# A two-layer decoder trunk: both feed-forward blocks in one matmul form, the residual's chunks turned a step ahead, two attention heads paired

## The chip, the cores and the metric

The kernel runs on one core of a Trainium2 chip. The metric is the device time of one execution in microseconds; the kernel before takes 2439.62 us, the median of three runs (2439.14 to 2440.86). Engines are named as the profile names them: PE is TensorE's matmuls and PEld its weight loads, DVE is VectorE, ACT is ScalarE, POOL is GpSimd, SP is SyncE, which issues the DMAs of the weights.

## What is computed

Two layers on a residual stream h of 256 positions by 2048 columns, each with three sub-layers in sandwich norms (cut from the reference):

```python
for l in range(DEPTH):                                   # DEPTH = 2
    xn = rms_norm(h, mix_pre_g[l])
    proj = jnp.einsum('bsd,dc->bsc', xn, w_in[l])
    qa, ka, va, cq, ckv, kidx, widx, cu, cv = jnp.split(proj, split_at, axis=-1)
    oa = diff_attention(...)                             # 6 heads of 128
    ob = dsa_attention(...)                              # 6 heads of 128
    oc = chunk_spatial_gating(gelu(cu), gelu(cv), ...)   # 512 columns: u * (W_s v + b)
    mix = concatenate([oa, ob, oc])
    h = h + rms_norm(jnp.einsum('bsc,cd->bsd', mix, w_out[l]), mix_post_g[l])
    xa = memory_attention(rms_norm(h, x_pre_g[l]), rms_norm(mem, mem_g[l]), ...)
    h = h + rms_norm(xa, x_post_g[l])
    ff = swiglu(rms_norm(h, f_pre_g[l]), f_w_gu[l], f_w_down[l])   # 2048 -> 2 x 5632 -> 2048
    h = h + rms_norm(ff, f_post_g[l])
```

## The kernel before

Everything stays in SBUF but the weights, which are streamed once. A matrix is used in f32 accuracy as a pair of rounded parts: hi is the value rounded to the matmul's type, lo what is left; a product is hi times hi, hi times lo and lo times hi, three matmuls. Chunks are 128 columns of h; KD is 16 of them.

The stream. plan() (from L263) lists the weights in the order of their use; loaded() lets SP load them in pieces of 1 MB, tile raw with three buffers; splits() cuts a piece into batches of 1024 elements a row, ACT copying hi (L206) and DVE subtracting for lo (L207). weights() hands batches to the matmuls. After each batch it splits ahead up to three batches (prefetch) and lets every waiting side job take one step (pump): side jobs are Python generators, appended with start(), and their steps fall where the matmuls of that batch stand in the program. Behind that, the Tile framework's scheduler fixes the order on each engine, with its own estimate of times, except where a stretch is put under manual_schedule: begin() does that for DVE and ACT from one of the residual's steps until the first weights after it are used up, and in that stretch weights() pumps first and splits ahead afterwards.

Forms of a matmul. mm_n gives rows: h's chunk is the stationary side, 512 weight columns move. mm_t gives the transposed output: a 128 by 128 block of weights is stationary and 256 positions move; a chunk and block takes lo with x's hi, hi with x's hi, and hi with x's lo, three matmuls of 256 columns with three weight loads, and four blocks (512 weight columns: two of the gate g, two of u) make a group. mm_w puts x's hi and lo side by side, so that a block's hi serves both in one matmul of 512 columns, with one of 256 for lo; the two halves of the result are added afterwards by add_up (ACT L425, DVE L427).

The feed-forward block (from L1237) takes its 5632 hidden columns in two halves of 11 groups, each group 256 hidden columns. Layer 1 and the first two groups of layer 0 go through mm_t; the other 20 groups of layer 0 through mm_w, two calls for a group, with side job act_w; its u is multiplied by the norm on POOL (L1279). g times u is POOL's (L1254).

The residual (L609) adds a normed sub-layer output og to H and turns H for the next sub-layer, two chunks at a time: turn_x (L588) transposes two chunks on PE (L593; tile xtp, one of two PSUM tiles each) and splits them (ACT L212, DVE L213, tile x). add is DVE's (L622), add_beside scales on ACT (L628) and adds on POOL (L629). Its argument bare tells that no other matmuls stand beside it: cross to FFN in both layers, FFN to the mix of layer 1. There the first matmuls come straight behind it, and 38 warming matmuls (L446) fill PE's wait for the norm's root. The mix to cross residual is not bare: the keys of the memory (t_k) run beside it. Each yield of it is a step, so one batch of weights.

The mix's end. The projections come in the order of the plan: heads 0 and 1, heads 2 and 3, head 4, the gating's values cv, head 5. attention_a (tiles qk, lga, pA, ptp, pva, oat) is a side job; oat (L1032) transposes a head's output into MX, and split_mx makes its two parts, tile mx or, for the first ones, m6. gating (L1077) is a side job on cv: gelu on ACT (L1082), a layer norm (last steps DVE L1093, POOL L1094), yp on PE, y on DVE (L1103), the product with u on POOL (L1105) into chunks 12 to 15 of MX. project_out multiplies MX with w_out in five columns; the first of them takes its chunks in the order of MIX_FIRST (chunk, count), so that the ones that are ready last are used last. turn_memory waits for the first column and the side jobs head_5 and chunks, and then transposes the memory (mp, mtp L477).

Of the kernel before, what the change touches and what calls it, by code (L numbers as in the profile page):

```python
# [21 lines left out]
P = 128  # L22
# [36 lines left out]
def trunk(ctx: ExitStack, tc, a, onehot, out):  # L59
# [200 lines left out]
    MIX_FIRST = ((8, 4), (0, 4), (6, 2), (12, 4), (4, 2))  # L260

    def plan():
# [7 lines left out]
        for l in range(L):  # L270
# [93 lines left out]
    def twice(gen):  # L364
        for _ in gen:
            if next(gen, gen) is gen:
                break
            yield

# [40 lines left out]

    def mm_w(nk, x):


        tiles = [acc.tile([P, 512], F32, tag="acc", name="acc") for _ in range(2)]
        for n, k, hi, lo in weights(nk, 256):
            for b in range(2):
                cs = slice(b * P, (b + 1) * P)
                mm(tiles[b], hi[:, cs], x[:, :, k, :], n == 0, False)
                mm(tiles[b][:, 0:256], lo[:, cs], x[:, 0, k, :], False, n == nk - 1)
        return tiles  # L420

    def add_up(dst, tiles):

        for b, t in enumerate(tiles):
            nc.scalar.activation(dst[:, b, :], t[:, 256:512], AF.Copy)  # L425
        for b, t in enumerate(tiles):
            nc.vector.tensor_tensor(dst[:, b, :], t[:, 0:256], dst[:, b, :], op=ALU.add)  # L427
# [160 lines left out]
    def turn_x(src, c, xh, xl, gain):  # L588

        for j, (pool, tag) in enumerate(((ps3, "tp"), (ps2, "lg"))):  # L590
# [3 lines left out]
            split(xh[:, c + j, :], xl[:, c + j, :], p[:, 0:256], gcol(gain[0], gain[1], c + j, KD))  # L594
# [14 lines left out]
    def residual(og, ss, evac, nxt, res, bare, off):  # L609


        rest = evac()
        r = row_rsqrt(ss)
# [5 lines left out]
        def add(c, n):  # L619
            f = slice(c * P, (c + n) * P)  # L620
            for t in range(2):
                nc.vector.scalar_tensor_tensor(H[:, t, f], og[:, t, f], r[:, t:t + 1], H[:, t, f],  # L622
                                               op0=ALU.mult, op1=ALU.add)

        def add_beside(c, n):
            f = slice(c * P, (c + n) * P)
            for t in range(2):
                nc.scalar.activation(og[:, t, f], og[:, t, f], AF.Copy, scale=r[:, t:t + 1])  # L628
                nc.gpsimd.tensor_tensor(H[:, t, f], H[:, t, f], og[:, t, f], op=ALU.add)  # L629
# [699 lines left out]
```

## Time and profile before

| what | value |
|---|---|
| median of three runs | 2439.62 us |
| the profiled execution's own time | 2439.03 us |
| its span, first to last instruction | 2437.3 us |
| PE busy | 2402.6 us (99%) |
| PEld busy | 2204.8 us (90%) |
| DVE busy | 1432.9 us (59%) |
| ACT busy | 1220.3 us (50%) |
| POOL busy | 260.5 us (11%) |
| moved by DMA | 453.11 MB, mean 186 GB/s |
| mean granted TensorE clock | 0.998 of full speed |

Busy is the time in which an engine had at least one instruction in work. Ends of matmuls are modelled, and neighbours overlap, so a single matmul's time is longer than its spacing; a rate is read from the spacing of starts or from the chain of waits. In a timeline, an entry in brackets is the engine's idle time ahead of the row and the engine and line that ended it; a row with x4 is four instructions of one kind in a row, with their time together.

### The profile page before, as it was taken

The numbers are of one execution on the slowest core, as the hardware profiler recorded it, in microseconds if no ns is written. First come the engines' busy times: TensorE is split into PE (matmuls) and PEld (weight loads), VectorE is DVE, ScalarE is ACT, GpSimd is POOL, SyncE is SP. The second block draws the span as 40 slices with busy tenths as digits, with TensorE's granted clock in tenths as the row PEclk, the third lists the DMA queues.
The fourth block names the chain that finished last, engine by engine and source line by source line (L and its number), as shares of the span: only waits on it lengthen the run. The fifth ranks groups of instructions, "written<-read, shape, count | busy, mean of one in ns | idle before, by whom it ended". The sixth has DMA issues, their size and how long they took to land.

```text
span 2437.3 us, 40157 instructions
## 1 busy us (share of the span) xinstructions
PE 2402.6 (99%) x16461; PEld 2204.8 (90%) x16461; DVE 1432.9 (59%) x2189; ACT 1220.3 (50%) x1858; POOL 260.5 (11%) x209
## 2 busy tenths in 40 slices
PE   9999999999999999999999999999999999999998
PEld 8899789998888988888899997898999989999987
DVE  5676767665554455555566767676655544555554
ACT  5655645564444444444455656455544444444443
POOL 0010131011110011111110101310100000000001
PEclk9999999999999999999999999999999999999999
DMA  7755475455555555555654555754555556555554
GB/s 245 241 172 156 160 264 180 149 182 189 183 183 192 188 188 190 190 182 181 193 178 151 172 156 165 241 171 141 191 192 196 196 195 187 194 191 194 196 190 130
DMA packets 363661, 453.11 MB, mean 186 GB/s; under 512 B 10011, under 2 KB 282325, under 8 KB 362965
## 3 DMA queue, kind: packets, MB, share of 16 engines
q1 hardware_dynamic: 361748, 443.45, 55.6%
q0 software_dynamic: 1248, 6.29, 0.8%
q8 instruction: 129, 2.11, 0.4%
q10 hardware_dynamic: 480, 0.80, 0.1%
q14 instruction: 56, 0.45, 0.1%
HBM read 444.72 MB, written 5.79 MB: 185 GB/s over the span
## 4 chain that ended last, share of the span: by engine, by line
PE 92%; DVE 4%; DMA 2%; ACT 1%; issue 1%; SPq 0%; POOL 0%; ACTq 0%; POOLq 0%; DVEq 0%
PE acc L201 87%; DVE lo L207 2%; PE ixp L201 1%; PE xtp L593 1%; DMA m<-in_mem_dram 1%; ACT hi L206 1%; PE lga L201 0%; DVE mx L207 0%; DVE H L622 0%; DMA H<-in_x_dram 0%; PE warm L446 0%; PE pvb L201 0%; PE pva L201 0%; PE lgx L201 0%; PE pvx L201 0%
## 5 line engine op out<-in xcount | busy, mean ns | idle before, releaser
L207 DVE TENSOR_TENSOR lo<-raw,hi 128x1024 fp32r<-128x1024 f32 (+2 forms) x839 | 1011.3, 1207 | 838.6 <-ACT hi L206 836.6
L206 ACT ACTIVATE hi<-raw 128x1024 fp32r<-128x1024 f32 (+2 forms) x839 | 860.3, 1026 | 958.8 <-PE acc L201 871.3
L201 PE MATMUL acc<-x,hi 128*128 128x256 f32 (+2 forms) x6080 | 1282.0, 303 | 0.0
L201 PEld LDWEIGHTS acc<-x,hi 128*128 128x128 f32 (+1 forms) x6080 | 963.8, 188 | 57.1 <-issue 2.0
L201 PE MATMUL acc<-x,lo 128*128 128x256 f32 x3680 | 939.0, 280 | 9.0 <-ACT x L212 4.9
L201 PEld LDWEIGHTS acc<-x,lo 128*128 128x128 f32 x3680 | 690.7, 188 | 20.5 <-ACT x L212 10.2
L201 PE MATMUL acc<-hi,hx 128*128 128x512 f32 (+1 forms) x1760 | 452.5, 347 | 0.0
L201 PEld LDWEIGHTS acc<-hi,hx 128*128 128x128 f32 x1760 | 308.6, 189 | 41.6 <-issue 0.2
L201 PE MATMUL acc<-lo,hx 128*128 128x512 f32 (+1 forms) x880 | 304.9, 347 | 0.0
L201 PEld LDWEIGHTS acc<-lo,hx 128*128 128x128 f32 x880 | 166.7, 189 | 20.8 <-issue 0.2
L201 PE MATMUL acc<-hi,mx 128*128 128x512 f32 (+1 forms) x576 | 148.5, 345 | 7.4 <-ACT mx L206 5.5
L1254 POOL TENSOR_TENSOR g<-g,u 128x512 f32<-128x512 f32 x44 | 84.5, 1921 | 589.2 <-ACT g L1264 587.6
L201 PEld LDWEIGHTS acc<-hi,mx 128*128 128x128 f32 x576 | 99.9, 190 | 21.1 <-ACT mx L206 6.5
L201 PE MATMUL acc<-hi,x 128*128 128x384 f32 (+1 forms) x384 | 109.2, 360 | 0.0
L201 PE MATMUL acc<-lo,mx 128*128 128x512 f32 (+1 forms) x288 | 98.6, 343 | 0.0
L1279 POOL TENSOR_TENSOR u<-u,rbh 128x512 f32<-128x512 f32 x20 | 26.1, 1307 | 505.1 <-DVE u L427 505.1
L201 PEld LDWEIGHTS acc<-hi,x 128*128 128x128 f32 x384 | 69.9, 188 | 7.0 <-issue 2.0
L201 PE MATMUL acc<-lo,x 128*128 128x384 f32 (+1 forms) x192 | 69.1, 360 | 0.0
L212 ACT ACTIVATE x<-xtp,gT 128x256 fp32r<-128x256 f32 x96 | 40.3, 471 | 43.4 <-PE xtp L593 43.4
L201 PEld LDWEIGHTS acc<-lo,mx 128*128 128x128 f32 x288 | 54.6, 190 | 6.1
L213 DVE SCALAR_TENSOR_TENSOR x<-xtp,gT,x 128x256 fp32r<-128x256 f32 x96 | 41.7, 475 | 18.9 <-ACT x L212 18.9
L201 PE MATMUL acc<-hi,cx 128*128 128x512 f32 (+1 forms) x160 | 42.8, 352 | 0.0
(254 smaller groups left out, 1981.9 us busy)
## 6 DMA issues: line engine op xcount, KB each, us to landing
raw<-in_f_w_gu_dram SPq DMA_DIRECT2D x192, 512.0 KB, 4.5
raw<-in_f_w_gu_dram SPq DMA_DIRECT2D x80, 1024.0 KB, 5.0
raw<-in_f_w_down_dram SPq DMA_DIRECT2D x76, 1024.0 KB, 5.1
raw<-in_w_out_dram SPq DMA_DIRECT2D x30, 1024.0 KB, 6.0
raw<-in_w_in_dram SPq DMA_DIRECT2D x48, 512.0 KB, 4.8
raw<-in_w_in_dram SPq DMA_DIRECT2D x23, 1024.0 KB, 5.3
raw<-in_x_wkv_dram SPq DMA_DIRECT2D x16, 1024.0 KB, 5.2
raw<-in_w_in_dram SPq DMA_DIRECT2D x12, 960.0 KB, 5.1
```

Of the source, the lines that this page charges most:

```text
L201: return nc.tensor.matmul(o, lhsT=lhsT, rhs=rhs, start=start, stop=stop, skip_group_check=True)
L206: nc.scalar.activation(hi, src, AF.Copy)
L207: eng.tensor_tensor(lo, src, hi.bitcast(F32), op=ALU.subtract)
L212: nc.scalar.activation(hi, src, AF.Copy, scale=scale)
L213: nc.vector.scalar_tensor_tensor(lo, src, scale, hi.bitcast(F32), op0=ALU.mult, op1=ALU.subtract)
L593: nc.tensor.transpose(p[:, t * P:(t + 1) * P], src[:, t, (c + j) * P:(c + j + 1) * P], ident)
L1254: nc.gpsimd.tensor_tensor(g, g, u, op=ALU.mult)
L1279: nc.gpsimd.tensor_tensor(u, u, two(fnx["rb"]), op=ALU.mult)
```

## The change

Three edits.

All FFN groups go through mm_t; mm_w, add_up, act_w and twice are gone, and the plan loads all FFN weights g and u together, as it did in layer 1.

The residual turns its chunks one step ahead: turn_x only transposes, split_x splits. Chunks 0 to 3 are turned in the steps ahead of the first matmuls, chunks 4 and 5 while the second batch is used, and so on. The adds of columns 8 to 15 stay on ACT and POOL only where the residual is not bare; in the bare ones DVE does them all. begin() runs two steps ahead instead of three in the bare case.

Heads 4 and 5 are one group of 512 weight columns in front of cv, and their attention is one side job, last_heads. The gating thus has no projection behind it and its steps fall into the first column of project_out. MIX_FIRST puts chunks 4 and 5 in front of 12 to 15; chunks() splits them when last_heads is done.

```diff
-    MIX_FIRST = ((8, 4), (0, 4), (6, 2), (12, 4), (4, 2))
+    MIX_FIRST = ((8, 4), (0, 4), (6, 2), (4, 2), (12, 4))
...
-            for h in range(0, 4, 2):
+            for h in range(0, 6, 2):
                 yield spec(pairs(w_qk, h * P, 256), KD, 512)
-            yield spec(pairs(w_qk, 4 * P, P), KD, 256)
             yield spec(rows(w_in, C_CV, 512), KD, 512)
-            yield spec(pairs(w_qk, 5 * P, P), KD, 256)
...
                 for j in range(0, nh, 2):
-                    if l or hf == 0 and j < 4:
-                        yield spec(pairs(a["f_w_gu"][l], (hf * nh + j) * P, 256), KD, 512)
-                    else:
-                        for c in range(2):
-                            yield spec(rows(a["f_w_gu"][l][:, c, :], (hf * nh + j) * P, 256), KD, 256)
+                    yield spec(pairs(a["f_w_gu"][l], (hf * nh + j) * P, 256), KD, 512)
...
         rest = evac()
+        if not bare:
+            prefetch()
         r = row_rsqrt(ss)
         if bare:
             warm(38)
         yield
...
+        def turn(c):
+            split_x(turn_x(H, c), c, xh, xl, nxt)
+
         add(0, 2)
-        turn_x(H, 0, xh, xl, nxt)
+        p = turn_x(H, 0)
+        add(2, 2)
+        split_x(p, 0, xh, xl, nxt)
+        turn(2)
+        add(4, 2)
         if bare:
-            prefetch(2)
-        add(2, 2)
+            prefetch()
         rest()
-        yield
-        turn_x(H, 2, xh, xl, nxt)
-        add(4, 4)
-        if bare:
-            prefetch(3)
-        yield
-        turn_x(H, 4, xh, xl, nxt)
-        add_beside(8, 4)
-        yield
-        turn_x(H, 6, xh, xl, nxt)
-        yield
-        turn_x(H, 8, xh, xl, nxt)
-        add_beside(12, 4)
-        yield
-        for c in range(10, KD, 2):
-            turn_x(H, c, xh, xl, nxt)
-            yield
+        add(6, 2)
+        yield
+        turn(4)
+        yield
+        turn(6)
+        add(8, 4, not bare)
+        yield
+        turn(8)
+        yield
+        turn(10)
+        add(12, 4, not bare)
+        yield
+        turn(12)
+        yield
+        turn(14)
+        yield
...
-        qk4 = qk_group(4, 1)
-        start(attention_a(qk4, 4, 1))
+        qk45 = qk_group(4, 2)
+
+        def last_heads():
+            yield from attention_a(qk45, 4, 2)
+        start(last_heads())
         t_cv = mm_n(KD, 512, xh, xl)
...
         start(gating())
-        qk5 = qk_group(5, 1)
         flush()
...
-        def head_5():
-            yield from twice(attention_a(qk5, 5, 1))
-            split_mx(place(4), 4)
-
         def chunks():
             split_mx(place(6), 6)
+            while any(g.__name__ == "last_heads" for g in side):
+                yield
+            split_mx(place(4), 4)
             while any(g.__name__ == "gating" for g in side):
                 yield
...
-        begin(residual(og, oss, evac, ("f_pre_g", l), nx, True, 64), 3, 0)
+        begin(residual(og, oss, evac, ("f_pre_g", l), nx, True, 64), 2, 0)
...
             for j in range(0, nh, 2):
-                if l or hf == 0 and j < 4:
-                    start(act(mm_t(KD, [P] * 4, xh, xl), j, hh, hl))
-                else:
-                    t_g, t_u = mm_w(KD, xx), []
-                    start(act_w(t_g, t_u, j, hh, hl))
-                    t_u += mm_w(KD, xx)
+                start(act(mm_t(KD, [P] * 4, xh, xl), j, hh, hl))
```

Three places show how instructions move. On DVE behind the cross sub-layer of layer 0 (H is an add to the residual, x the lo part of a turned chunk, lo that of a weight batch, og the last output column), before:

```order
L622 SCALAR_TENSOR_TENSOR H<-og,rs_r,H 128x256 x2
L213 SCALAR_TENSOR_TENSOR x<-xtp,gT,x 128x256 x2
L622 SCALAR_TENSOR_TENSOR H<-og,rs_r,H 128x256 x2
L701 TENSOR_TENSOR og<-acc,gX 128x256 x2
L213 SCALAR_TENSOR_TENSOR x<-xtp,gT,x 128x256 x2
L622 SCALAR_TENSOR_TENSOR H<-og,rs_r,H 128x512 x2
L207 TENSOR_TENSOR lo<-raw,hi 128x1024
L213 SCALAR_TENSOR_TENSOR x<-xtp,gT,x 128x256 x2
L207 TENSOR_TENSOR lo<-raw,hi 128x1024
L213 SCALAR_TENSOR_TENSOR x<-xtp,gT,x 128x256 x2
L207 TENSOR_TENSOR lo<-raw,hi 128x1024
```

and now, from the same place:

```order
L604 SCALAR_TENSOR_TENSOR H<-og,rs_r,H 128x256 x4
L213 SCALAR_TENSOR_TENSOR x<-xtp,gT,x 128x256 x4
L604 SCALAR_TENSOR_TENSOR H<-og,rs_r,H 128x256 x2
L207 TENSOR_TENSOR lo<-raw,hi 128x1024
L683 TENSOR_TENSOR og<-acc,gX 128x256 x2
L604 SCALAR_TENSOR_TENSOR H<-og,rs_r,H 128x256 x2
L213 SCALAR_TENSOR_TENSOR x<-xtp,gT,x 128x256 x2
L207 TENSOR_TENSOR lo<-raw,hi 128x1024
L213 SCALAR_TENSOR_TENSOR x<-xtp,gT,x 128x256 x2
L604 SCALAR_TENSOR_TENSOR H<-og,rs_r,H 128x512 x2
L207 TENSOR_TENSOR lo<-raw,hi 128x1024
L213 SCALAR_TENSOR_TENSOR x<-xtp,gT,x 128x256 x2
```

Four adds stand ahead of the first x, two pairs of x follow one another, and of the 512-column adds that POOL had, DVE now has one pair here and the other three rows below the last shown.

PE at the same place, behind the warming matmuls (xtp are the transposes, acc the first group), before:

```order
L446 MATMUL warm<-wz 128x256 x38
L593 MATMUL xtp<-ident,H 128x128 x4
L201 MATMUL acc<-x,lo 128x256
L201 MATMUL acc<-x,hi 128x256
L201 MATMUL acc<-x,lo 128x256
L201 MATMUL acc<-x,hi 128x256
```

and now:

```order
L416 MATMUL warm<-wz 128x256 x38
L564 MATMUL xtp<-ident,H 128x128 x8
L201 MATMUL acc<-x,lo 128x256
L201 MATMUL acc<-x,hi 128x256
L201 MATMUL acc<-x,lo 128x256
L201 MATMUL acc<-x,hi 128x256
```

Eight transposes stand ahead of the first matmul, four more than before; the next four have moved into the second batch.

PE in the first output column at the end of the mix of layer 0 (oat transposes attention heads' outputs, yp is the gating's matmul, mx the parts of MX); before, the end of the column, where the last head's transposes stand, with yp far ahead of it:

```order
L201 MATMUL acc<-lo,mx 128x512
L201 MATMUL acc<-hi,mx 128x512
L1032 MATMUL oat<-ident,o_3332 128x128 x2
L201 MATMUL acc<-hi,mx 128x512
L201 MATMUL acc<-lo,mx 128x512
L201 MATMUL acc<-hi,mx 128x512
L201 MATMUL acc<-lo,mx 128x512
L201 MATMUL acc<-hi,mx 128x512
L201 MATMUL acc<-lo,mx 128x512
L201 MATMUL acc<-hi,mx 128x512
L201 MATMUL acc<-lo,mx 128x512
L477 MATMUL mtp<-ident,mp 128x128 x8
```

and now, in the middle of the column, with 24 matmuls behind the last row ahead of the next transposes (mtp):

```order
L201 MATMUL acc<-hi,mx 128x512
L1014 MATMUL oat<-ident,o_3079 128x128 x4
L201 MATMUL acc<-hi,mx 128x512
L201 MATMUL acc<-lo,mx 128x512
L201 MATMUL acc<-hi,mx 128x512
L201 MATMUL acc<-lo,mx 128x512
L201 MATMUL yp<-wsT,vg 128x128 x2
L201 MATMUL acc<-hi,mx 128x512 x3
L201 MATMUL acc<-lo,mx 128x512
L201 MATMUL acc<-hi,mx 128x512 x2
L201 MATMUL acc<-lo,mx 128x512
L201 MATMUL acc<-hi,mx 128x512
L201 MATMUL yp<-wsT,vg 128x128 x6
```

Both last heads' transposes stand ahead of the gating's yp, and the gating's chunks are the last ones of the column.

## Rows read from the trace of the kernel before

**Rows 1.** the page: span, and PE's busy time, share and instructions

```profile
span 2437.3 us, 40157 instructions
...
PE 2402.6 (99%) x16461; PEld 2204.8 (90%) x16461; DVE 1432.9 (59%) x2189; ACT 1220.3 (50%) x1858; POOL 260.5 (11%) x209
```

**Rows 2.** windows (us, each engine's busy us and instructions), both FFNs

```profile
905.00:1085.50 180.50, 180.50 (x1024) 156.85 (x1024) 101.41 (x112) 84.92 (x112) 27.72 (x16) 1.00 0.56 186
...
2107.90:2282.00 174.10, 174.10 (x1539) 174.10 (x1538) 93.52 (x89) 76.34 (x80) 14.11 (x9) 1.00 0.59 194
```

**Rows 3.** POOL's timeline (start, us, line, operation, [idle before]), FFNs' second halves

```profile
882.45 1.31 POOL L1279 TENSOR_TENSOR u<-u,rbh 128x512 f32<-128x512 f32 x1 [140.52 <-DVE u L427]
...
1108.31 1.29 POOL L1279 TENSOR_TENSOR u<-u,rbh 128x512 f32<-128x512 f32 x1 [19.04 <-DVE u L427]
...
2086.11 1.76 POOL L1254 TENSOR_TENSOR g<-g,u 128x512 f32<-128x512 f32 x1 [141.48 <-ACT g L1264]
...
2303.70 1.76 POOL L1254 TENSOR_TENSOR g<-g,u 128x512 f32<-128x512 f32 x1 [20.00 <-ACT g L1264]
```

**Rows 4.** windows behind two bare residuals, cross to FFN and FFN to mix

```profile
480.50:504.40 23.90, 21.56 (x180) 20.40 (x179) 17.01 (x26) 14.14 (x25) 7.66 (x6) 1.00 0.44 150
...
1232.40:1256.50 24.10, 21.79 (x178) 20.43 (x179) 16.75 (x25) 14.15 (x25) 6.95 (x4) 1.00 0.45 157
```

**Rows 5.** PE's timeline, cross to FFN in layer 0

```profile
481.59 0.39 PE L201 MATMUL acc<-x,lo 128*128 128x256 f32 x1 [0.46 <-ACT x L212]
...
493.29 0.44 PE L593 MATMUL xtp<-ident,H 128*128 128x128 f32 x2 [0.46 <-POOL H L629]
...
494.46 0.36 PE L201 MATMUL acc<-x,lo 128*128 128x256 f32 x1 [0.74 <-DVE lo L207]
```

**Rows 6.** chain of waits (start, us, what), residual and layer 1's mix end

```profile
501.17 2.74 PE acc L201 x24
...
503.91 0.44 PE xtp L593 x4
...
1511.62 8.22 PE acc L201 x36
```

**Rows 7.** DVE's timeline, cross to FFN in layer 0

```profile
479.35 0.88 DVE L622 SCALAR_TENSOR_TENSOR H<-og,rs_r,H 128x256 f32<-128x256 f32 x2
...
486.27 1.41 DVE L622 SCALAR_TENSOR_TENSOR H<-og,rs_r,H 128x512 f32<-128x512 f32 x2
...
487.59 1.22 DVE L207 TENSOR_TENSOR lo<-raw,hi 128x1024 fp32r<-128x1024 f32 x1
...
492.13 2.18 DVE L207 TENSOR_TENSOR lo<-raw,hi 128x1024 fp32r<-128x1024 f32 x1 [1.66 <-ACT hi L206]
```

**Rows 8.** PE by line, 250 to 312 us (two) and 1470 to 1530

```profile
L201 PE MATMUL acc<-hi,mx 128*128 128x512 f32 x57 | 18.8, 400 | 3.8 <-ACT mx L206 2.9 <-DVE mx L207 0.9
...
L477 PE MATMUL mtp<-ident,mp 128*128 128x128 f32 x8 | 1.1, 276 | 0.6 <-DMA mp<-in_mem_dram 0.6
...
L201 PE MATMUL acc<-hi,mx 128*128 128x512 f32 x63 | 20.6, 398 | 3.6 <-ACT mx L206 2.7 <-DVE mx L207 0.9
```

**Rows 9.** timelines of ACT, POOL and DVE, the gating's chain in layer 0

```profile
258.10 0.69 ACT L1082 ACTIVATE vg<-acc,rs_r 128x512 f32<-128x512 f32 x1
...
271.33 3.83 POOL L1094 TENSOR_TENSOR vg<-vg,lnb 128x512 f32<-128x512 f32 x2 [104.33 <-PE oat L1032]
...
287.26 3.50 POOL L1105 TENSOR_TENSOR MX<-MX,y 128x512 f32<-128x512 f32 x2 [12.10 <-DVE y L1103]
...
286.76 0.75 DVE L1103 TENSOR_TENSOR y<-yp,bsb 128x256 f32<-128x256 f32 x2
...
289.54 1.77 DVE L207 TENSOR_TENSOR mx<-MX,mx 128x512 fp32r<-128x512 f32 x1
```

**Rows 10.** timelines of DVE and PE, mix to cross in layer 0

```profile
379.02 5.09 DVE L622 SCALAR_TENSOR_TENSOR H<-og,rs_r,H 128x256 f32<-128x256 f32 x6
...
386.49 0.36 PE L201 MATMUL acc<-mh,lo 128*128 128x256 f32 x1 [1.47 <-DVE lo L207]
```

More of the change, by code (lines that the diff above doesn't have):

```diff
@@ L362, in prefetch @@
             ready.append(x)
[L364 to L367, printed above, removed]
-            yield
     def weights(nk, cols, hold=False):
@@ L409, in mm_t @@
         return tiles
[L411 to L427, printed above, removed]
     def mm_n(nk, cols, xh, xl, hold=False):
@@ L586, in row_rsqrt, with turn_x @@
         return rsqrt(sr, 2, 1.0 / D)
-    def turn_x(src, c, xh, xl, gain):
+    def turn_x(src, c):
+        ps = []
         for j, (pool, tag) in enumerate(((ps3, "tp"), (ps2, "lg"))):
@@ L593, in turn_x, with split_x @@
                 nc.tensor.transpose(p[:, t * P:(t + 1) * P], src[:, t, (c + j) * P:(c + j + 1) * P], ident)
-            split(xh[:, c + j, :], xl[:, c + j, :], p[:, 0:256], gcol(gain[0], gain[1], c + j, KD))
+            ps.append(p[:, 0:256])
+        return ps
+    def split_x(ps, c, xh, xl, gain):
+        for j, p in enumerate(ps):
+            split(xh[:, c + j, :], xl[:, c + j, :], p, gcol(gain[0], gain[1], c + j, KD))
     def pre_norm(res):
@@ L617, in residual, with add @@
         res["x"] = xh, xl, _ = new_x("x", off)
[L619 removed]
+        def add(c, n, beside=False):
             f = slice(c * P, (c + n) * P)
             for t in range(2):
[L622 to L629, printed above, removed]
[L631 to L632 removed]
+                if beside:
+                    nc.scalar.activation(og[:, t, f], og[:, t, f], AF.Copy, scale=r[:, t:t + 1])
+                    nc.gpsimd.tensor_tensor(H[:, t, f], H[:, t, f], og[:, t, f], op=ALU.add)
+                else:
+                    nc.vector.scalar_tensor_tensor(H[:, t, f], og[:, t, f], r[:, t:t + 1], H[:, t, f],
+                                                   op0=ALU.mult, op1=ALU.add)
+        def turn(c):
+            split_x(turn_x(H, c), c, xh, xl, nxt)
+        add(0, 2)
+        p = turn_x(H, 0)
[3 more added lines that the diff above has]
+        add(4, 2)
         if bare:
[L634 to L635 removed]
+            prefetch()
         rest()
+        add(6, 2)
         yield
[L638 to L641 removed]
+        turn(4)
         yield
[L643 to L644 removed]
+        turn(6)
+        add(8, 4, not bare)
         yield
[L646 removed]
+        turn(8)
         yield
[L648 to L649 removed]
+        turn(10)
+        add(12, 4, not bare)
         yield
[L651 to L653 removed]
+        turn(12)
+        yield
+        turn(14)
+        yield
         yield from pre_norm(res)
@@ L1142, in turn_memory @@
         def turn_memory():
-            while used[0] == at or any(g.__name__ in ("head_5", "chunks") for g in side):
+            while used[0] == at or any(g.__name__ in ("last_heads", "chunks") for g in side):
                 yield
@@ L1251, in trunk @@
             hh, hl = hx[:, 0], hx[:, 1]
-            def hidden(g, u, j, hh, hl):
-                nc.gpsimd.tensor_tensor(g, g, u, op=ALU.mult)
-                yield
-                split(flat(hh[:, j:j + 2, :]), flat(hl[:, j:j + 2, :]), flat(g))
             def act(t_gu, j, hh, hl):
@@ L1265, in act @@
                 nc.vector.tensor_tensor(u, v2(t_gu[1]), two(fnx["rb"]), op=ALU.mult)
-                yield from hidden(g, u, j, hh, hl)
-            def act_w(t_g, t_u, j, hh, hl):
-                while "rb" not in fnx:
-                    yield
-                g = wk.tile([P, 2, 256], F32, tag="res", name="g", bufs=3)
-                add_up(g, t_g)
-                nc.vector.tensor_tensor(g, g, two(fnx["rb"]), op=ALU.mult)
-                nc.scalar.activation(g, g, AF.Silu)
-                while not t_u:
-                    yield
-                u = wk.tile([P, 2, 256], F32, tag="res", name="u", bufs=3)
-                add_up(u, t_u)
-                nc.gpsimd.tensor_tensor(u, u, two(fnx["rb"]), op=ALU.mult)
-                yield from hidden(g, u, j, hh, hl)
-            for j in range(0, nh, 2):
-                if l or hf == 0 and j < 4:
-                    start(act(mm_t(KD, [P] * 4, xh, xl), j, hh, hl))
-                else:
-                    t_g, t_u = mm_w(KD, xx), []
-                    start(act_w(t_g, t_u, j, hh, hl))
-                    t_u += mm_w(KD, xx)
+                nc.gpsimd.tensor_tensor(g, g, u, op=ALU.mult)
+                yield
+                split(flat(hh[:, j:j + 2, :]), flat(hl[:, j:j + 2, :]), flat(g))
+            for j in range(0, nh, 2):
+                start(act(mm_t(KD, [P] * 4, xh, xl), j, hh, hl))
             finish()
@@ L1301, in trunk @@
             cur = {}
-            begin(residual(og, oss, evac, ("mix_pre_g", l + 1), cur, True, 64), 3, 0)
+            begin(residual(og, oss, evac, ("mix_pre_g", l + 1), cur, True, 64), 2, 0)
         else:
```

3 lines of the change are left out of this document (1 added, 2 removed).

## The prediction

> **What bounds the kernel now.** I read the page first [rows 1]: PE is busy for 2402.6 of 2437.3 us. So the end is set by PE's work and by the 35 us in which PE stands still, and everything else counts only where PE waits for it. Then I read the windows of the two feed-forward forms [rows 2], where PE has no idle time at all, so there only the number and kind of matmuls counts; next the starts of one POOL product per group of 256 hidden columns (u times the norm in layer 0, g times u in layer 1), whose spacing is the period of a group [rows 3]; and then the places where PE does wait: the stretches behind the bare residuals [rows 4 to 7] and the end of the mixing sub-layer [rows 6, 8, 9]. The last is the one residual that is not bare [rows 10]. The execution shown took 2439.03 us, 1.7 more than its span and 0.59 less than the median of the runs (2439.62); nothing of the change lies outside the span.
>
> **Part 1, one form for both FFNs.** In layer 0, 20 of the 22 groups go through mm_w: nine of the first half (j from 4 on), all eleven of the second. POOL's product L1279 starts at 882.45 for the first group of the second half and at 1108.31 for its last, ten periods: 22.586 us each. In layer 1 the same place in mm_t form runs from 2086.11 to 2303.70, ten periods of 21.759 [rows 3]. The saving is 0.827 us a group. The windows say why: mm_w issues 1024 matmuls in 180.50 us, 176.3 ns on average, 128 a group, 22.56 us; mm_t 1539 in 174.10, 113.1 ns, 192 a group, 21.72 [rows 2]. One 512-column and one 256-column matmul together take 352.9 ns (22.586/64), three of 256 columns 340.0. The price of the change is half as many weight loads again (192 for 128); in the second row PEld is at 174.10 of 174.10 us, so they run beside the matmuls without gap, and that time already holds them. Gone as well are add_up's copies and adds and POOL's product with the norm; in the first row DVE is at 101 and ACT at 85 of 180 us, so that work was covered and its loss is worth nothing. 20 x 0.827 = **-16.5 us**. Bounds: the windows' periods give 0.84 (-16.8), and -15 is left for a group at either seam that does not see the whole period.
>
> What speaks against it is a page of the Trainium skill, "TensorE: Matmul & The Clock Gate", section "Back-to-back issue gap": an isolated matmul costs its columns over 2.4 plus 2.5 ns, so a fixed cost per matmul favours few wide ones. By it the pair would take 324.8 ns and the three 327.5, so an estimate by that page makes the group 0.2 us longer. The trace disagrees in sign (352.9 against 340.0); the price above is the trace's.
>
> **Part 2, three bare residuals** (cross to FFN in both layers, FFN to the next mix). In layer 0 PE starts its first matmul at 481.59, after the first four transposes, and the chain shows batch 6's last four transposes ending at 504.35 [rows 5, 6]: 22.76 us. Of that six batches of 24 matmuls at 2.74 are 16.44, and 28 transposes at 0.11 (0.44 for four) are 3.08. The other 3.24 are waits: several of the kind that stands ahead of 481.59 (0.46; each step of two chunks is transposed right before it is used, so PE stands while ACT copies it), 0.46 for H from POOL at 493.29, and 0.74 for DVE's lo at 494.46. The last has its cause in the DVE rows [rows 7]: the lo at 492.13 takes 2.18 us where the one at 487.59 took 1.22, while POOL adds H (7.66 us busy in this window [rows 4]).
>
> After the change, by the order, eight transposes stand in front of the first matmul, the next four inside batch 2, and so on one step ahead; all adds are DVE's, and POOL has none. The four extra transposes in front fill the 0.46 that PE waited for ACT ahead of 481.59, so they add nothing, and 24 stay inside: 16.44 + 24 x 0.11 + two remaining waits of that kind, 0.92, = 20.0. The gain is 2.8. Is DVE able to? It now does 16 adds' worth: from 479.35, with 0.44 for an add of 256, 0.7 for one of 512, the add's 0.44 for an x piece of the same 256, 1.22 for a lo [rows 7], the lo for batch 4 ends near 485.4, for batch 5 near 489.1, for batch 6 near 492.6, while PE needs them near 491, 494 and 496.6. That is ahead by some four us, and the x of each step by about 1.5. So the adds moved to DVE cost nothing while that lead lasts; if it goes, each batch waits for up to one lo, 1.2. Layer 1's stretch has the same shape, and the FFN to mix one idles about as much (24.10 - 21.79 = 2.31 against 23.90 - 21.56 = 2.34 [rows 4]); there the first matmul may come 0.2 later. 2.8 + 2.8 + 2.6 = **-8.2 us**, from -9.7 (no wait left) to 0 (rival D).
>
> **Part 3, mix to cross residual.** It hides behind the memory's keys, and the order there hardly changes. DVE's first adds become eight of 256 instead of four of 256 and two of 512: 8 x 0.44 - (4 x 0.44 + 2 x 0.7) = +0.3, with the lo that PE waits for behind them (1.47 at 386.49; the adds take 5.09 there [rows 10]). PE gets that lo later: **+0.5 us** for both layers, 0 to 1.2.
>
> **Part 4, heads 4 and 5 paired ahead of the gating's values.** PE's work is the same; only waits change. Before, PE waits 3.8 us for mx and 0.6 for the memory chunk in layer 0, and 3.6 for mx in layer 1, most of it for ACT's part of the split [rows 8]. Afterwards heads 4 and 5 are projected before cv, so nothing but the first output column stands between cv's end and the gating's chunks. By the order PE then has 84 matmuls of 512 columns before chunk 12's first; 36 take 8.22 us with [rows 6], 0.228 each, so 19.2, and the small ones (pva, oat, yp) about 1.7: a cover of 20.9. Against it the gating's chain from gelu at 258.10: vg is added by 271.33 + 3.83 = 275.16, which is 17.1; then, where the order puts yp, up to 8 matmuls ahead (1.8), yp 0.9 (eight of the transposes' 0.11), one weights' lo on DVE ahead of y (1.2), y 0.75, POOL's first half of 3.50 (1.75), mx hi 0.7 (as the gelu of the same shape on ACT) and mx lo 1.8 as at 289.54 [rows 9]. Sum 26.0. PE waits 5.1 in each layer instead of 4.4 and 3.6: **+2.2 us**. In the low case (no queueing: 17.1 + 0.9 + 0.75 + 1.75 + 0.7 = 21.2) the cover holds but for 0.3, and what stays is ACT's split behind the last heads' transposes, some 2 us of the 2.9 and 2.7 now: -4. In the high case the chain lasts as before, from 258.10 to the mx lo's end at 291.31, 33.2: 12.3 a layer, +16.6.
>
> Sum: -16.5 - 8.2 + 0.5 + 2.2 = -22.0. 2439.03 - 22.0 = 2417.0 in the profiled execution's terms, 2417.6 in the median's.
>
> **Rivals.** B, the gating's chain keeps its 33 us: some of it was waiting in PE's and DVE's queues (y starts at 286.76, 11.6 us after vg is there) and that speaks against; for it, that DVE has the pair's softmax in the same stretch. 2417.6 - 2.2 + 16.6 = 2432.0. C, the chain is fast and the waits halve: 2417.6 - 6.2 = 2411.4. For it speaks the 21.2 above, against it POOL's 1.9 us a piece and the weights' lo in DVE's queue. D, turning ahead brings nothing, since the waits go from H and x to the weights' lo on a DVE that is now the busiest beside PE: 2417.6 + 8.2 = 2425.8; against it the four us of lead. E, a pair of one wide and one narrow matmul costs no more than three narrow ones, since the columns are the same 768, and layer 0's longer period belongs to its stretch, not to the form: then part 1 brings nothing and the time is 2417.6 + 16.5 = 2434.1. Against it: the stretch shows PE busy throughout, and tiles, weights and places are those of layer 1 [rows 2, 3]. The Trainium skill's page cited above points this way. F, slower: layer 0 must now stream a group's 4.19 MB in 21.76 us, 193 GB/s, where it moved 186 [rows 2]. If transfers limited it below 181 GB/s a group would take 23.1, +0.53 x 20 = +10.6 instead of -16.5, and with -5.5 from the rest the time passes 2444.5, 0.2% above the median. That is one price and one threshold, but layer 1 moves 194 GB/s with PE never idle and the transfer engines busy to 0.59 [rows 2].
>
> **How the numbers follow.** Forecast 55% (its own range 2412 to 2423), C 14%, D 14%, B 13%, E 2%, F 2%. The range reaches over C and D, from 2409 (the median with -16.8, -9.7, 0 and -4) to 2428, and leaves out B, E and F. A measurement of this kernel tells 0.2%, 4.9 us, from no change: the forecast, B, C and D are all faster than 2434.7 (96%), E lies on that line and is counted as within (2%), F is slower (2%).
>
> **What would show it.** In layer 0's second half, g x u on POOL every 21.76 us instead of 22.59, with PEld full; if it stays above 22, part 1 is wrong. Behind the warming matmuls, first matmul to the end of batch 6's transposes about 20.0 us, no PE wait for H, and every lo on DVE near 1.2; waits for lo instead mean D. At the end of the mix, PE's waits for mx near 5 us a layer, put down to POOL's product or its split; 2 means C, 12 B. A wait of PE in places that I have not listed, or of transfers, would make the forecast wrong as a whole.

## The result

The changed kernel takes 2425.74 us, the median of four runs (2423.88 to 2426.98), where the kernel before took 2440.24 on the same chips (2439.14 to 2441.37): a ratio of 0.994, 95% interval 0.9923 to 0.9957. It is 14.5 us faster. The forecast was 2417.6, 22.0 us faster; the time lies in the range of 2409 to 2428, and the direction was right, but a third of the gain is missing. The experiments put it in its places: one part of the change brings all that it was to bring, one brings half, and two cost more than they were to cost.

### The profile after

The page of the profiled execution of the changed kernel (2425.12 us), first lines, as in [rows 1]:

```profile
span 2423.4 us, 42616 instructions
...
PE 2389.2 (99%) x17741; PEld 2249.2 (93%) x17741; DVE 1412.6 (58%) x2129; ACT 1188.7 (49%) x1764; POOL 201.9 (8%) x177
```

The span is 13.9 us shorter, and PE's busy time fell by 13.4. A busy share does not tell where. For that the program was cut at points that both kernels have, each the start of one matmul in PE's timeline, and the pieces were set side by side (us):

| from | to | before | after | difference | forecast |
|---|---|---|---|---|---|
| start | last matmul of the sparse attention, layer 0 | 186.22 | 184.25 | -1.97 | 0 |
| there | first product with the memory, layer 0 (the mix's end) | 186.78 | 188.27 | +1.49 | +0.7 |
| there | first product with x (mix to cross) | 26.65 | 29.38 | +2.73 | +0.25 |
| warming matmuls, layer 0 | first product with the hidden values | 259.53 | 250.58 | -8.95 | -7.4 and -2.8 |
| there | the same of the second half | 369.90 | 360.83 | -9.07 | -9.1 |
| warming matmuls, FFN to mix | last norm of the mix's inputs | 69.71 | 68.50 | -1.21 | -2.6 |
| last matmul of the sparse attention, layer 1 | first product with the memory | 181.69 | 183.74 | +2.05 | +1.5 |
| there | first product with x | 26.75 | 29.34 | +2.59 | +0.25 |
| warming matmuls, layer 1 | first product with the hidden values | 251.92 | 250.59 | -1.33 | -2.8 |

All other pieces agree within 0.02 us, but for the end behind the last FFN, which is 0.2 us shorter after. The first line holds nothing that the change touches; the windows of the same stretch, before and after, show another granted clock there, 0.50 and 1.00. In this stretch every execution traced here differed (153.1 to 154.9 us from the first norm on, and 30.2 to 33.5 ahead of it), so its 2 us are an accident of the two executions and no gain.

```profile
10.00:16.00 6.00, 4.99 (x24) 4.73 (x24) 3.76 (x7) 5.24 (x11) 0.00 (x0) 0.50 1.05 389
```

```profile
10.00:16.00 6.00, 4.31 (x38) 4.08 (x37) 3.75 (x7) 5.16 (x11) 0.00 (x0) 1.00 1.05 389
```

**The FFN.** POOL's timeline after (the product g times u of the first and last group of layer 0's second half), then the window of that half (us, each engine's busy us and instructions, PEclk, DMA share, GB/s):

```profile
873.93 1.76 POOL L1243 TENSOR_TENSOR g<-g,u 128x512 f32<-128x512 f32 x1 [141.47 <-ACT g L1241]
...
1091.54 1.76 POOL L1243 TENSOR_TENSOR g<-g,u 128x512 f32<-128x512 f32 x1 [20.00 <-ACT g L1241]
```

```profile
900.00:1080.00 180.00, 180.00 (x1591) 180.00 (x1590) 95.98 (x90) 78.98 (x83) 14.08 (x8) 1.00 0.59 194
```

Ten periods of 21.761 us, against 22.586 in [rows 3]. PE and PEld are both full, and the transfers move 194 GB/s where they moved 186 in [rows 2]: layer 0 is now layer 1 over again.

**The mix to cross residual.** DVE (its eight adds, then the first four and the last four of them by themselves), POOL, ACT and PE after, layer 0, then the window behind PE's wait and the one after that:

```profile
378.55 7.40 DVE L604 SCALAR_TENSOR_TENSOR H<-og,rs_r,H 128x256 f32<-128x256 f32 x8
...
378.55 1.68 DVE L604 SCALAR_TENSOR_TENSOR H<-og,rs_r,H 128x256 f32<-128x256 f32 x4
...
380.14 5.81 DVE L604 SCALAR_TENSOR_TENSOR H<-og,rs_r,H 128x256 f32<-128x256 f32 x4
...
385.87 2.35 DVE L207 TENSOR_TENSOR lo<-raw,hi 128x1024 fp32r<-128x1024 f32 x2
```

```profile
379.94 5.73 POOL L602 TENSOR_TENSOR H<-H,og 128x512 f32<-128x512 f32 x4 [3.60 <-ACT og L601]
...
379.15 1.32 ACT L601 ACTIVATE og<-og,rs_r 128x512 f32<-128x512 f32 x2
```

```profile
387.23 0.55 PE L201 MATMUL acc<-mh,lo 128*128 128x256 f32 x1 [2.68 <-DVE lo L207]
387.59 0.42 PE L201 MATMUL acc<-mh,hi 128*128 128x256 f32 x1
```

```profile
387.20:390.40 3.20, 3.17 (x15) 3.20 (x16) 3.20 (x6) 0.42 (x2) 0.00 (x0) 0.50 0.18 61
390.40:393.60 3.20, 3.20 (x29) 3.20 (x29) 1.26 (x2) 1.83 (x3) 0.00 (x0) 0.99 0.71 266
```

DVE runs eight adds in a row and needs 7.40 us for them, 0.93 each on average; the lo stands behind them. The average hides two rates: the four that start ahead of POOL's first add take 1.68 us together, the four that run beside POOL's adds 5.81, although all are of one shape. ACT's scaling of og is no reason, for it already runs beside two of the quick ones. PE waits 2.68 us, where it waited 1.47 in [rows 10]. And then PE goes on at half speed: in the 3.2 us behind the wait the granted clock is 0.50, the lower of its two levels, 1.2 GHz, and 15 matmuls are in work where 29 are in the next 3.2 us. In the kernel before, the same window behind its shorter wait has a clock of 1.00:

```profile
386.40:389.60 3.20, 3.11 (x27) 3.14 (x28) 3.20 (x4) 1.75 (x6) 1.09 (x1) 1.00 0.00 0
```

The wait grew by 1.2 us, and 1.5 more were lost behind it: together the 2.73 of the table. A pass with the same wait and a clock of 1.00, shown below, puts 1.3 of the 1.5 down to the slow matmuls.

**A bare residual.** PE after (cross to FFN in layer 0), and the chain of waits at its end (start, us, what):

```profile
504.11 0.39 PE L201 MATMUL acc<-x,lo 128*128 128x256 f32 x1 [0.24 <-ACT x L212]
...
516.01 0.39 PE L201 MATMUL acc<-x,lo 128*128 128x256 f32 x1 [0.73 <-DVE lo L207]
```

```profile
506.09 0.95 ACT hi L206
507.04 0.62 ACT sqj L550 x2
...
507.68 0.73 ACT sqj L550 x2
...
509.91 0.95 ACT hi L206
510.87 0.62 ACT sqj L550 x2
...
513.75 0.96 ACT hi L206
...
514.73 1.24 DVE lo L207
...
516.01 4.03 PE acc L201 x33
```

From the first matmul at 483.83 to the end of batch 6's transposes it takes 20.04 us, where 20.0 was forecast, and there is no wait for H. Batch 7 starts at 504.11, 20.28 us behind the first matmul; before it started 22.51 us behind, so 2.2 us are gained up to here. But twelve microseconds later PE waits for lo, and the chain says for whom that lo waited: not for DVE, as the brackets of the row suggest, but for ACT, which runs four of the next norm's squares (sqj, each a pair of rows in the chain) between two hi.

**The mix's end.** PE by line after (250 to 312 us, layer 0), the row of mx as in [rows 8]:

```profile
L201 PE MATMUL acc<-hi,mx 128*128 128x512 f32 x56 | 18.4, 401 | 4.0 <-DVE mx L207 2.0 <-ACT mx L206 1.9
```

With 0.29 before a yp that makes 4.28 us of waits, against the 5.1 that were forecast and 4.36 before, and 4.21 in layer 1 (3.60 before). Yet the piece is longer by 1.49 and 2.05. So in layer 0 PE's waits for mx are none of the price of this part, and in layer 1 a third of it; an experiment below shows more.

### The profile page after: what moved, and what is told of

Its sections match the earlier page's. It is cut to its first block, busy times and chain, and to the rows that moved or that the text cites. A ratio compares the mean times of both kernels' runs of the same rounds, so it can differ in the third digit from the quotient of the medians.

```text
span 2423.4 us, 42616 instructions
## 1 busy us (share of the span) xinstructions
PE 2389.2 (99%) x17741; PEld 2249.2 (93%) x17741; DVE 1412.6 (58%) x2129; ACT 1188.7 (49%) x1764; POOL 201.9 (8%) x177
## 4 chain that ended last, share of the span: by engine, by line
PE 91%; DVE 4%; ACT 2%; DMA 2%; issue 1%; SPq 0%; POOL 0%; ACTq 0%; POOLq 0%; DVEq 0%
PE acc L201 86%; DVE lo L207 2%; ACT hi L206 1%; PE xtp L564 1%; PE ixp L201 1%; ACT sqj L550 1%; PE lga L201 1%; DMA m<-in_mem_dram 1%; DVE H L604 1%; DMA H<-in_x_dram 0%; DVE mx L207 0%; PE warm L416 0%; DMA lp<-in_a_lambda_dram 0%; PE pvb L201 0%; PE lgx L201 0%
## 5 line engine op out<-in xcount | busy, mean ns | idle before, releaser
L207 DVE TENSOR_TENSOR lo<-raw,hi 128x1024 fp32r<-128x1024 f32 (+2 forms) x839 | 1000.9, 1194 | 870.7 <-ACT hi L206 868.4
L201 PE MATMUL acc<-x,hi 128*128 128x256 f32 (+1 forms) x7360 | 1270.0, 277 | 0.0
L201 PEld LDWEIGHTS acc<-x,hi 128*128 128x128 f32 (+1 forms) x7360 | 1111.2, 188 | 2.8 <-issue 2.7
L201 PE MATMUL acc<-x,lo 128*128 128x256 f32 x3680 | 889.5, 278 | 6.8 <-DVE lo L207 4.6
L201 PEld LDWEIGHTS acc<-x,lo 128*128 128x128 f32 x3680 | 690.1, 188 | 13.4 <-DVE lo L207 6.1
L1243 POOL TENSOR_TENSOR g<-g,u 128x512 f32<-128x512 f32 x44 | 76.6, 1741 | 1131.3 <-ACT g L1241 1131.3
L201 PEld LDWEIGHTS acc<-lo,x 128*128 128x128 f32 x192 | 36.1, 188 | 3.9 <-issue 1.3
```

Source lines behind the costliest of these rows:

```text
L201: return nc.tensor.matmul(o, lhsT=lhsT, rhs=rhs, start=start, stop=stop, skip_group_check=True)
L207: eng.tensor_tensor(lo, src, hi.bitcast(F32), op=ALU.subtract)
L1243: nc.gpsimd.tensor_tensor(g, g, u, op=ALU.mult)
```

## The experiments

Times are medians of four runs each, against the kernel before on the same chip (2438.7 to 2440.0). Because granted clocks differ from run to run at the places named below, medians of like kernels move by a microsecond or two; the pieces of the table above are the finer measure, and both are given.

### One form alone

```diff
-                    if l or hf == 0 and j < 4:
-                        yield spec(pairs(...), KD, 512)
-                    else: ...
+                    yield spec(pairs(a["f_w_gu"][l], (hf * nh + j) * P, 256), KD, 512)
```

The loop that uses the weights calls mm_t for every group in the same way.

> The kernel before with the first edit alone: every FFN group of layer 0 in mm_t form. If the form's price is the period read from the traces (22.59 against 21.76 us a group), 20 groups bring -16.5 us against the kernel before, and the spacing of POOL's products in layer 0 is 21.76 us. If the other two edits of the changed kernel carry part of what its FFN stretch shows (its length there shrank by 16.6), this one brings less, below -14.

2422.64 us (2421.86 to 2423.14), ratio 0.9929, interval 0.9914 to 0.9944: -17.3. The piece with nine groups shrank from 259.53 to 252.10, 0.826 a group; the one with eleven from 369.90 to 360.83, 0.825. Part 1 is worth its 16.5 us and needs nothing of the other edits. It also means that the rest of the change, taken together, costs 3 us: this kernel is faster than the changed one.

### The mix to cross residual as before

```diff
+        if not bare:
+            add(0, 2); turn(0); add(2, 2); rest()
+            yield
+            turn(2); add(4, 4)
+            yield
...
```

The prefetch that the change put ahead of this residual's norm goes as well.

> The changed kernel with the residual from mix to cross as it was before (adds and transposes in the old order), the bare residuals as changed. Theory: this residual lost the changed kernel 2.7 us in each layer: DVE runs eight adds of 256 in a row (0.86 us each beside POOL), so the lo that PE waits for comes 1.2 us later, the wait grows to 2.7, and behind it the granted clock is at 0.50 for some 3 us, another 1.5. Undone, the wait is 1.5 again, the clock stays at 1.00 and the time falls by 5.3 us to about 2420.4. Rival: the loss lies in the mix end (heads paired) and only shows up here because PE comes earlier by half a microsecond: then the wait stays above 2 us and the time falls by under 2.

2423.33 us (2421.06 to 2424.74), ratio 0.9933, interval 0.9916 to 0.9949: 2.4 under the changed kernel, half of what was expected. The pieces in question did just what the theory says: 26.87 and 26.88 us instead of 29.38 and 29.34, with PE's wait back at 1.47. The other half went elsewhere: the mix's end of layer 1 took 185.56 us in this execution, 1.8 more than in the changed kernel with the same code, and there the clock fell between its two waits for mx (0.50 from about 1490 to 1497 us). The rival, that the loss only shows up here, falls.

### All adds of that residual on DVE

```diff
-        add(8, 4, not bare)
+        add(8, 4)
-        add(12, 4, not bare)
+        add(12, 4)
```

> The changed kernel with all of the adds of the mix to cross residual on DVE, none on ACT and POOL. If it is POOL's adds beside DVE's that stretch these (0.86 us each instead of 0.44), the eight adds end after 3.5 us instead of 7.3, the lo comes before PE asks for it, the wait of 2.7 us goes with the fall of the clock behind it, and the segment falls from 29.4 to about 25.3: 8 us less, to about 2417.5. If DVE's adds are slow for another reason, they stay near 0.86 and the segment stays or grows.

2418.39 us (2416.42 to 2418.96), ratio 0.991, interval 0.9893 to 0.9926: 7.3 under the changed kernel. DVE's timeline and the window of PE's former wait:

```profile
381.51 3.26 DVE L604 SCALAR_TENSOR_TENSOR H<-og,rs_r,H 128x256 f32<-128x256 f32 x8
384.68 1.22 DVE L207 TENSOR_TENSOR lo<-raw,hi 128x1024 fp32r<-128x1024 f32 x1
385.81 2.74 DVE L604 SCALAR_TENSOR_TENSOR H<-og,rs_r,H 128x512 f32<-128x512 f32 x4
```

```profile
384.00:390.40 6.40, 6.40 (x57) 6.40 (x56) 6.40 (x11) 6.37 (x16) 0.00 (x0) 1.00 0.19 68
```

The same eight adds take 3.26 us instead of 7.40 once POOL does not add beside them; the four of 512 that POOL had cost DVE 2.74. Giving DVE all of the work makes it done sooner. This edit takes ACT's scaling away together with POOL's adds; that POOL is the cause follows from the two rates of the eight adds in the changed kernel. That both write H is not the reason: a lo, which has other tiles, is slowed too (2.18 us beside POOL's add against 1.22 in [rows 7]). PE does not wait at all, and the pieces fall to 24.87 and 24.63, two microseconds under the kernel before. The Trainium skill says of this, in "SBUF — State Buffer", section "SBUF: two separate sides", that a DVE instruction with two inputs in SBUF and a GpSimd one that reads SBUF take their shared ports in turn, each for a whole instruction; the adds, with og and H as inputs, agree (1.45 us each beside POOL's, 0.41 alone).

### The wait filled

```diff
+            if fill and n == fill[0]:                    # n == 8 of the memory's keys
+                for _ in range(fill[1]):                 # 20
+                    mm(outs[0], wz[:, 0:P], wz, False, False)
```

> The changed kernel with 20 matmuls of ones put into the products with the memory's keys, where PE waits 2.7 us for lo (the keys of the first cross head are off by a constant, so the output is not the reference's; the work is otherwise the same). They fill 2.3 us of that wait and remove nothing of what causes it. If the granted clock falls because PE stands still there, it stays at 1.00 now, and the segment of 29.4 us becomes 27.9 (the 1.5 us per layer that the slow matmuls cost come back: -3 us, 2422.7). If the clock falls for another reason, the segment stays at 29.4.

2425.41 us (2424.0 to 2426.48), ratio 0.9941, interval 0.9926 to 0.9956. PE's timeline, and the window behind the fill:

```profile
386.86 2.55 PE L201 MATMUL acc<-wz 128*128 128x256 f32 x20
389.77 0.36 PE L201 MATMUL acc<-mh,lo 128*128 128x256 f32 x1 [0.37 <-DVE lo L207]
...
391.21 0.44 PE L567 MATMUL xtp<-ident,H 128*128 128x128 f32 x2 [0.50 <-DVE x L213]
```

```profile
389.70:392.90 3.20, 2.62 (x21) 2.46 (x22) 3.20 (x6) 1.60 (x6) 0.00 (x0) 1.00 0.20 54
```

The clock does what was expected: DVE and POOL do what they did (eight adds in 7.48 us), PE is kept at work, and the clock stays at 1.00 in both layers. The size was wrong: the piece stays at 29.5, which the expectation gave to the rival. With the fill PE still waits 0.37 for lo, the scheduler moves transposes behind it forward, and PE meets a new wait of 0.50 for x there; the piece behind it is 0.76 shorter. The net is 0.6 a layer, and the median cannot tell it from nothing.

### The squares spread

```diff
             for t in range(2):
                 square(H[:, t, i * 512:(i + 1) * 512], ss[:, t, i:i + 1])
-            if i % 2:
-                yield
+            yield
```

> The changed kernel with pre_norm's squares spread over four steps instead of two (one pair of 512 columns a step), everywhere. Theory: in the bare residuals PE now comes to the end of the stretch earlier, but ACT has four squares (3 us) in one step ahead of the next weights' hi, and PE waits 0.73 us for lo at 516.01, 1250.20 and 1714.45; spread, ACT has 2.5 us of work to a batch of 2.7 and the wait goes: -2.2 us, to about 2423.5. Rival: the norm comes two steps later and the first groups' products wait for it: no change or up to +2.

2424.32 us (2421.21 to 2426.08), ratio 0.9935, interval 0.992 to 0.995: -1.4, unclear by itself. The pieces behind the three bare residuals shrank from 250.58, 68.50 and 250.59 to 249.43, 67.22 and 249.42, by 1.2 each, 3.6 in all; but the mix's ends took 189.76 and 185.37 us, 1.5 and 1.6 more than in the changed kernel, the clock at 0.50 for some of it in both layers. Against the kernel with one form alone (252.10, 69.87, 251.99) the bare residuals have now gained 2.67, 2.65 and 2.57 us: 7.9, and the forecast for them was 8.2.

### Heads apart

```diff
-    MIX_FIRST = ((8, 4), (0, 4), (6, 2), (4, 2), (12, 4))
+    MIX_FIRST = ((8, 4), (0, 4), (6, 2), (12, 4), (4, 2))
...
-        qk45 = qk_group(4, 2)
...
+        qk4 = qk_group(4, 1)
+        start(attention_a(qk4, 4, 1))
         t_cv = mm_n(KD, 512, xh, xl)
...
         start(gating())
+        qk5 = qk_group(5, 1)
```

The plan's order, head_5 and chunks() go back with it.

> The changed kernel with heads 4 and 5 apart, head 5 behind the gating's values, and the old MIX_FIRST. Theory: the pairing costs 1.5 us in layer 0 and 2.05 in layer 1 (from the last dsa product to the first product with the memory), so undone it brings -3.5 us, to about 2422.2. Rival: the pairing is neutral, as PE's listed waits say (4.3 and 4.2 us against 4.4 and 3.6), and the difference is elsewhere: within 1 us of 2425.7.

2422.74 us (2421.44 to 2425.18), ratio 0.9931, interval 0.9916 to 0.9946: 3.0 under the changed kernel, near the 3.5 of the theory. In the traced execution the pieces, 186.66 and 182.92, are 1.6 and 0.8 shorter; another 1.3 us of it come from the clock in the pass shown below, which is luck and not the heads.

PE in layer 0: the matmuls for the logits of the differential heads (lga). First the changed kernel, head 4 and then head 5 of the pair; then this run, head 5 apart:

```profile
250.09 0.93 PE L201 MATMUL lga<-qk 64*128 64x128 f32 x8
250.94 0.50 PE L201 MATMUL acc<-lo,x 128*128 128x512 f32 x1
...
255.29 0.92 PE L201 MATMUL lga<-qk 64*128 64x128 f32 x4
256.14 0.74 PE L201 MATMUL acc<-hi,x 128*128 128x512 f32 x2
...
257.26 0.92 PE L201 MATMUL lga<-qk 64*128 64x128 f32 x4
258.11 0.50 PE L201 MATMUL acc<-hi,x 128*128 128x512 f32 x1
```

```profile
276.44 0.49 PE L201 MATMUL lga<-qk 64*128 64x128 f32 x4
276.86 0.49 PE L201 MATMUL yp<-wsT,vg 128*128 128x128 f32 x2
277.28 0.70 PE L201 MATMUL lga<-qk 64*128 64x256 f32 x4
277.91 0.38 PE L201 MATMUL yp<-wsT,vg 128*128 128x128 f32 x1
```

By the spacing of starts, head 4's eight matmuls hold PE for 0.85 us, and head 5's, of the same shapes, for 0.85 and 0.85 again, 1.70; apart, head 5's hold it for 0.42 and 0.63, 1.05. So 0.65 of the 1.5 and of the 2.05 us is PE's own time for the second head of the pair, in every paired kernel here. The trace shows how: head 4's matmuls, and head 5's when apart, start in twos, 7 ns from one another, as the code issues the two halves of 64 rows in turn. In the second head of a pair they start one by one, 0.1 to 0.3 us from one another, with other products between the first four and the last four. Heads 1 and 3 pay the same in every kernel. Which edit would keep the twos together was not tried.

This run also holds a pass in which the mix to cross wait was as long as in the changed kernel and the clock did not fall. PE's rows and the windows behind them, layer 0 and layer 1 of this execution:

```profile
386.89 0.36 PE L201 MATMUL acc<-mh,lo 128*128 128x256 f32 x1 [2.68 <-DVE lo L207]
```

```profile
386.80:390.00 3.20, 3.11 (x26) 3.15 (x27) 3.20 (x6) 0.48 (x3) 0.00 (x0) 1.00 0.20 60
```

```profile
1583.23 0.36 PE L201 MATMUL acc<-mh,lo 128*128 128x256 f32 x1 [2.74 <-DVE lo L207]
```

```profile
1583.20:1586.40 3.20, 3.17 (x16) 3.20 (x17) 3.20 (x6) 0.40 (x2) 0.00 (x0) 0.56 0.19 66
```

Over all runs, the clock fell behind 5 of the 6 waits of 2.7 us at this place, behind none of the ten of 1.5, and behind neither of the two filled places.

### Both repairs, heads paired and apart

These two put together edits shown above: the mix to cross residual as before and the squares spread, in the second also the heads apart.

> The changed kernel with the old residual from mix to cross and the squares spread over four steps; heads 4 and 5 stay paired. By the segments of the earlier runs the first takes 2.5 us off each layer (29.4 to 26.9 us from the first memory product to the first of x), the second 1.2 off each of three bare residuals: 2425.7 - 5.0 - 3.6 = 2417.1. If the squares only move the wait elsewhere, 2420.

> As the kernel beside it, with heads 4 and 5 apart and the old MIX_FIRST, so that only the one FFN form, the bare residuals turned ahead and the spread squares are left of the edits. If the pairing costs what the segments from the last dsa product to the first memory product show (1.6 and 0.8 us against the changed kernel, more where the clock falls between the mx waits), this one is 2.4 to 5 us faster than the kernel beside it, about 2414. If the pairing is neutral, both are the same.

2419.18 us (2417.96 to 2421.42), ratio 0.9917, interval 0.9902 to 0.9931, and 2415.99 us (2415.28 to 2417.22), ratio 0.9903, interval 0.9888 to 0.9918. The first missed its 2417.1 by two, although the pieces came as expected (26.88 and 26.87; 249.63, 67.43 and 249.43) and the clock fell in neither mix end of its traced execution. The four runs' mean clocks go from 0.996 to 0.999, so a fall in the slower ones is likely, but these were not traced. The pairing costs 3.2 us here.

### All that helps

Again edits from above, put together: the adds on DVE and the squares spread, in the first also the heads apart.

> One FFN form, bare residuals turned ahead, squares one pair a step, all adds of the mix to cross residual on DVE, heads 4 and 5 apart with the old MIX_FIRST. Against the run with the old adds (2415.99) the two segments behind the first memory product go from 26.7 to 24.8 us each: 2412. If the gain of the adds on DVE depended on the pairing, it stays at 2416.

> The same with heads 4 and 5 paired ahead of the gating's values. The pairing has cost 3 us in both comparisons so far (2425.74 against 2422.74, 2419.18 against 2415.99): 2415. If it was the neighbourhood of the other waits that made it dear, both are alike.

2411.75 us (2408.66 to 2412.09), ratio 0.9885, interval 0.9868 to 0.9901; and with the heads paired 2416.04 us (2414.83 to 2418.38), ratio 0.9908, interval 0.9893 to 0.9923. The first is 27 us faster than the kernel before and 14 faster than the changed one. The pairing costs 4.3 us in this comparison, more than before, and the windows of layer 1's mix end show where most of it lies in these two executions, 3.8 us by the pieces (first paired, second apart):

```profile
1486.00:1493.00 7.00, 5.47 (x18) 4.38 (x16) 2.73 (x2) 0.40 (x1) 2.18 (x1) 0.51 0.49 164
```

```profile
1484.00:1491.00 7.00, 5.94 (x28) 4.67 (x29) 5.38 (x7) 4.18 (x10) 1.65 (x1) 1.00 0.76 264
```

18 matmuls are in work in seven microseconds, or 28. Paired, PE waits twice within four microseconds (1.95 us for ACT's part of mx, then 1.3 to 2.0 for DVE's), with eight matmuls between; apart, two shorter waits of 0.7 to 0.9 lie close together, and the one of 1.95 comes some 13 us later. Of the 14 paired mix ends in these runs 6 show a piece of clock 0.50, and then last 189.8 to 190.0 us in layer 0 and 185.4 to 185.6 in layer 1, against 188.1 to 188.4 and 183.7 to 183.9 without; of the 10 that are apart 4 show one, half as long, and all ten last 186.7 to 188.6 and 181.7 to 183.3. On average over the executions the pairing costs 1.4 and 2.1 us.

## Why the prediction was half right

**Part 1 was right**, in mechanism and in size: -16.5 forecast, 20 groups times 0.825 measured, and alone in a kernel -17.3. The period of a stage that PE fills, read as the spacing of a once-a-group instruction over ten groups, carried over to the other layer to a few nanoseconds. Rival E falls with the run that makes this edit alone. With it falls, for these matmuls, the estimate from the Trainium skill's "TensorE: Matmul & The Clock Gate", section "Back-to-back issue gap", that few wide ones are cheaper (by its formula the pair is 325.0 ns and not the 324.8 of the prediction, which changes nothing).

**Part 2 was right where it was worked out and not worked out to its end.** The replay of PE up to the end of batch 6's transposes gave 20.0 us and 20.04 were measured; DVE's lead was there. Some of this is luck: of the 3.24 us that the prediction calls waits, PE's rows list 1.89 as idle, and the rest was spacing between transposes and products, a part of which went too. The step that failed is the check on who else must keep up: the lead was counted for DVE alone. ACT has the next norm's squares in the batches behind, four in a step, 3 us of work beside a hi of 1.04 in a batch of 2.7, and when PE comes 2.2 us earlier it runs into them. In layer 0 the 2.2 us gained up to batch 7 lose 0.73 to that wait. Of the gain of 8.2 us, 1.52, 1.37 and 1.40 were left (4.3, against one form alone), and with the squares spread it came to 7.9. Rival D had a part of this (a wait for lo takes the place of the others), but named DVE's queue, and it is ACT's.

**Part 3 was the worst term:** +0.5 forecast, +2.73 and +2.59 measured. The price of 0.44 us for an add came from [rows 7], a stretch in which POOL was idle at that moment; the row for this very place, 5.09 us for six in [rows 10], says 0.85 and was quoted without being used. At 0.85 the two more adds ahead of the lo put it 1.7 us later in each layer, not the 0.3 of the prediction; measured were 2.3 (7.40 for eight against 5.09 for six), since the two stand beside POOL's adds. The lo itself gained 1.1 of that back, as POOL is done by then (1.2 us instead of 2.3), and the wait grew by 1.2. The rest, 1.5 a layer, lies behind the longer wait, 1.3 of it in the clock, and no row of the kernel before shows a fall of the clock at this place.

**Part 4 had the direction and not the reason.** +2.2 forecast, +1.49 and +2.05 measured, of which waits of PE make -0.08 and +0.61. The gating's chain was a little faster than the replay (4.28 and 4.21 us of waits against 5.1). The step that failed is "PE's work is the same": the second head's logits take 0.65 us more in each layer. The rest, 0.9 and 0.8 us, is spread over the spacing of the products around them and was not traced to a cause. Rivals B (12 us of waits) and C (2) did not come.

The account: -16.5, -4.1 in the pieces of the bare residuals (with 4.3 against one form alone), +5.3, +3.5 and -2.0 at the start, which is no part of the change, add up to -13.7; with the 0.2 us at the very end they are the span's -13.9. So the time stands in the range although one part brought half and two cost more; no error made up for another, but in the traced execution 2 us of the gain are the accident at the start.

## What to carry to other kernels

A term that moves work to an engine is to be priced with the row of that very place, with what runs beside it there: an add that took 0.41 us alone took 1.45 beside another engine's adds, and taking the helper away made the whole faster. When a stretch is to become shorter, walk on past its end with every engine's queue, not only the one that gets the work: what used to be done in time may be what is late next. And a wait of PE that grows from 1.5 to 2.7 us can cost more than its length, since PE may go on at half its clock behind it.

## What was not expected of the hardware

In the traced executions the granted clock was 0.50 for some 3 us behind most of PE's waits of 2.7 us; for some 7 us, from between the two on, at six of the fourteen pairs of waits of 1.3 to 2.0 with eight matmuls between; for some 3 us behind a pair of waits of 0.7 to 0.9 in three of the ten mix ends that are apart, and once behind a single wait of 1.95. It was 1.00 behind waits of 1.5 that stood alone, and stayed so where matmuls of no use filled the wait. The same wait of 2.68 us cost 1.3 us less in the one pass in which the clock did not fall (28.09 against 29.38 us for the piece). Since it falls in some executions and not in others, kernels with such waits scatter by a microsecond or two; the kernel before, in whose one traced execution it did not fall between the start and the last FFN, scatters too (2437.33 to 2442.57 us in seven runs on one chip, the mean clock 0.999 and 0.996). What decides in a given pass was not found out.

That eight small matmuls of 64 rows take 0.85 us when they start in twos and 1.70 when they start one by one was not expected either; whether a head is the second of a pair decided it here.
